# A wide opening over four k-tiles, earlier rotation tables, closer tap pacing, and a third fast pair at the end of a hybrid attention and convolution block

## The chip, the core and the metric

The kernel runs on one core of one Trainium2 chip. The metric is the device time of one launch in microseconds. TensorE (PE) multiplies, VectorE (DVE), ScalarE (ACT) and GpSimd (POOL) do the elementwise work, and SyncE (SP) issues most transfers. "The clock" below is the TensorE clock that the chip granted, as the profile shows it.

## What is computed

One layer on 256 rows of width 2048, all in float32. Only the shape of the work matters here:

```python
xn    = rms_norm(x, norm1_g)
proj  = xn @ w_in                          # 2048 x 5120: q, k, v, and two halves of a gated unit
q, k  = rope(rms_norm(q)), rope(rms_norm(k))
att   = rms_norm(diff_attention(q, k, v))  # 4 heads, each the difference of two softmaxes
u     = silu(layer_norm(causal_depthwise_conv(ga * sigmoid(gg), 31 taps)))
h     = x + concat(att, u) @ w_out         # 2048 x 2048
hn    = rms_norm(h, norm2_g)
y     = h + (silu(hn @ w_gate) * (hn @ w_up)) @ w_down   # hidden width 5632
```

## The kernel before

**Three products for one.** Every matrix operand is split into a rounded upper part (`hi`) and the remainder (`lo`). A k-tile (128 rows of a weight) times both row halves of the 256 rows (m = 0, 1) for one block of 512 columns takes six matmuls of 512 columns: `xhi*whi`, `xlo*whi` and `xhi*wlo`, each for both m (lines 364, 365 and 370). Per piece of weight, ACT casts `whi` (line 325) and DVE subtracts `wlo = raw - whi` (line 334). For some pieces ("by DMA") ACT writes `-whi` into `wlo` instead (line 328), and a transfer issued by POOL adds `raw` to it (line 329), so DVE has nothing to do.

**Chunks.** All weight work is a list of chunks in the order PE takes them. Before each chunk's matmuls, `run_chunks` emits the loads, casts and subtractions of the next ones: one chunk ahead in the opening (the first nine chunks), later two, or three casts and two subtractions ahead near a fast pair. There are five `raw` buffers, three of `whi` and three of `wlo`. SP takes its transfers in this order, one after the other, and a load waits there until its buffer is free. A chunk normally holds 512 KB: two k-tiles of 512 columns.

**The opening.** The first block of `w_in` (512 columns, 16 k-tiles) is cut into chunks of 1, 1, 2, 2, ... k-tiles. The transposed input `xt` is loaded between the weights as `XLOADS` says (before chunk 0 k-tile 0, before chunk 1 k-tiles 1 to 3, and so on), and `x_split` (lines 238 and 239) makes `xhi` on ACT and `xlo` on DVE. `x_norm` squares and adds the k-tiles in place, PE sums over partitions (line 495), and POOL makes the first norm's factor per row half.

**Side work in `w_in`.** `w_in` has ten blocks: four for the gated unit, four for k and q, two for v. What follows a block runs in generators that go one step on at each half chunk (`resume`). The convolution is 8 channel tiles of 30 taps on DVE (line 553). They sit in queues, and `run_side` emits them after each half chunk as long as a credit is positive: every half chunk adds `KTILE_US`, a tap takes away `TAP_US`, a `wlo` 0.568 per k-tile, and other DVE work what its author estimated. After the last tap, `conv_back` waits some half chunks, transposes `y` (line 574), normalizes, transposes again (line 611), and ACT and DVE make the operands `mchi` and `mclo` (lines 615 to 619) that `w_out` needs for its k-tiles 8 to 15. The tables that rotate q and k are made by POOL from `rt` and `gb` (lines 199 to 205), in `late_constants`.

**Gate, up and down.** The hidden width is taken in groups of 4, 4 and 3 blocks of 512. Each group is followed by its passes over `w_down`: for i = 0 and 1, one fast block gives 1024 of the 2048 output columns. A fast block has pairs (`s`), seven-product forms of 2 x 2 tiles with 21 matmuls, and plain chunks of two k-tiles for the left (`g`) or right (`u`) 512 columns, 12 matmuls each. One pair covers what one `g` and one `u` cover together. For a pair DVE makes four sums (lines 1019 to 1021) and the remainders `wlb` and `wlt` (1028 and 1029), ACT casts `wh` (1022 and 1025). The pairs' weights (`wb`, 1 MB) have two buffers; the sums have one. The order of the chunks is a string. In the last group, with 12 k-tiles, both blocks have two pairs: `gguusggsuu`, then `gggsgsuuuu`. The left-hand forms for the pairs are made by `make_down_forms` from copies of the activations (`raw_act`), 11 DVE operations per group.

**Results.** After a block's last chunk that is not `u`, `down_half` adds up the banks (lines 1156 to 1163) and POOL adds the left columns to `h` in DRAM by transfer (line 1210); `down_whole` does the rest (lines 1226 and 1238). Before the last block, the last 1024 columns of `h` are fetched (`hend`, line 1200), and the last block adds into them and writes the output.

Of the kernel before, what the change touches and what calls it, by code (L numbers as in the profile page):

```python
# [15 lines left out]
ALU = mybir.AluOpType  # L16
# [33 lines left out]

WARM = 17

XLOADS = {0: range(0, 1), 1: range(1, 4), 3: range(4, 8), 5: range(8, 12), 7: range(12, 16)}
XSQUARES = 4

XWHOLE = 40

FIRST_CUTS = (1, 1)
OPENING = KD // NK + 1

CONV_TILES = 2

# [5 lines left out]
COPY_LAG = 2  # L68
HL_BUFS = 3

KTILE_US = 1.30
TAP_US = 0.396
CHAIN_US = 0.127
LO_US = 0.568
# [12 lines left out]


HD = N // P
NDS = (4, 4, 2)  # L90
DORDERS = {4: (ORDER, ORDER), 3: ("gguusggsuu", "gggsgsuuuu")}
HD_LAG = 3
DOWN_BY_DMA = {4: (dict(g=(0, 1), u=(1,)),) * 2, 3: (dict(g=(), u=()),) * 2}

Q1, Q6, Q7, Q5, Q2, Q4, Q3, QX = range(8)

# [31 lines left out]
def tile_block(  # L128
# [52 lines left out]
    def late_loads():  # L181
        sp.dma_start(out=cw.rearrange("p c w -> p (c w)"), in_=conv_w)
        for t, v in ((gb, vecs[:2]), (lamv, vecs[2:])):
            sp.dma_start(out=t, in_=v.rearrange("(o v) d -> o v d", o=1).to_broadcast(list(t.shape)))
        sp.dma_start(out=rt, in_=rope.rearrange("(m p) c d -> p m c d", p=P))

    def late_constants():
        late_loads()
        while not normed:
            yield  # L190
        yield from lag(16)
        act.mul(cols[:, AT["sg"] : AT["sg"] + 2], cols[:, AT["sg"] : AT["sg"] + 2], 1.0 - LAMBDA_INIT)

        act.mul(gb[:, 0, :], gb[:, 0, :], 1.0 / math.sqrt(DH))
        hd = DH // 2
        for i, key in enumerate("qk"):
            for m in range(NM):
# [57 lines left out]
    def lag(n):  # L255
        for _ in range(n):
            yield
# [14 lines left out]
    def spend(us):  # L272
        credit[0] -= us
# [72 lines left out]
    def multiply(c):  # L346
# [42 lines left out]
        if c["done"]:  # L389
            start(c["done"](ps))  # L390

    def run_chunks():
        n = len(chunks)
        i = j = 0
        pairs = [k for k in range(n) if chunks[k].get("kind") == "s"]
        raws = [k for k in range(n) if chunks[k].get("kind") != "s" and not chunks[k].get("spare_raw")]
        loaded, split = set(), set()

        def load(k):
            if k not in loaded:  # L400
# [12 lines left out]
        def freed(side, t):  # L413

            which, bufs = ((raws, RAW_BUFS), (pairs, PAIR_BUFS))[side]
            if not ahead[side] or pairs[2] - 1 not in loaded:
                return None
            k = which[place[side][ahead[side][0]] - bufs]
            return k if k in split and (t >= k or not chunks[k]["by_dma"]) else None

        def load_freed(t):
            while True:
                ready = [(k, side) for side in range(2) if (k := freed(side, t)) is not None]
                if not ready:
                    return
                load(ahead[min(ready)[1]].pop(0))

        for t in range(n):
            hi_lead, lo_lead = lead(t)
            while j < min(i, t + 1 + lo_lead):  # L430
                split_next()
                j += 1
            load_freed(t)
            while i < min(n, t + 1 + hi_lead):
                load(i)
                for which in ahead:
# [19 lines left out]
    rstd1 = [const.tile([P, 1], F32, tag=f"rstd1_{m}", name=f"rstd1_{m}") for m in range(NM)]  # L456

    eps1 = [const.tile([P, 1], F32, tag=f"eps1_{m}", name=f"eps1_{m}") for m in range(NM)]

    def square_sum(src, accum, **kw):  # L460
        junk = pre.tile([P, N], F32, tag="junk", name="junk", bufs=1)
# [20 lines left out]
    def x_norm():  # L482
# [13 lines left out]
        yield  # L496
        ss = small.tile([P, NM], F32, tag="ss1", name="ss1")
        act.copy(ss, ps[:, :NM])
        for m in range(NM):
            rsqrt_mean(rstd1[m], ss[:, m : m + 1], -D / 2, EPS)  # L500
            pool.tensor_scalar(eps1[m], ss[:, m : m + 1], -2.0 * EPS / D, EPS * EPS, ALU.mult, ALU.add)
        yield
        normed.append(True)

# [14 lines left out]
    def glu_done(c0, nct, ps):  # L519
# [11 lines left out]
        for m in range(NM):  # L531
            u = pre.tile([P, HN], F32, tag="wt", name="u", bufs=4)
            dve.scalar_tensor_tensor(u[:, :w], ps[m][:, w:], rstd1[m], sig[m][:, :w], ALU.mult, ALU.mult)
            us.append(u)
        spend(0.25)
        yield from lag(3 if c0 else 1)
        yield from room(1)
# [29 lines left out]
    def conv_back(b):  # L567
# [32 lines left out]
        for b in range(2):  # L600
            for m in range(NM):
                act.activation(ytok[m, b], ytok[m, b], AF.Identity, bias=lnb[:, m : m + 1], scale=lnr[:, m : m + 1])
            yield
        for b in range(2):
            for t in range(NB // 2):
                yield from room(1)
# [254 lines left out]
    def transposed(j, aa):  # L861
        last = j + 1 in FIRSTS and NDS[group_of(j)[0]] < HD
        b = j - group_of(j)[1]
        for t in range(N // P // 2):
# [9 lines left out]
            if b < 2 and 2 * t < nd:  # L874
                if not b and not t:
                    raw_act[g] = ffn["pool"].tile([P, 2, nd, S], F32, tag="draw", name="raw_act")
                act.copy(raw_act[g][:, b, 2 * t : 2 * t + 2, :], pt)
                yield from lag(3 if last else 6)
                if b and 2 * t + 2 == nd:
                    start(make_down_forms(g))  # L880
                continue
            hi, lo = lhs_two("a", j * (N // P) + 2 * t)
            act.copy(hi, pt)
            yield from lag(1 if last else 2)
# [250 lines left out]

    def down_pass(g, j0, nb):
        k0 = j0 * HD
        nd = NDS[g]
        ks = [k for k in range(nb * HD) if k >= 2 * HD or k % HD >= nd]
        twos = [dict(ks=(k0 + a, k0 + b), rows=slice(k0 + a, k0 + b + 1, b - a), k=i)  # L1140
                for i, (a, b) in enumerate(zip(ks[::2], ks[1::2]))]
        for i, order in enumerate(DORDERS[nb]):
            n = 2 * i
            end = {}
            fast_block(order, [dict(p=p, rows=slice(k0 + p, k0 + p + HD + 1, HD)) for p in range(nd)], twos,
# [48 lines left out]
    def fetch_end():  # L1194

        t = ffn["pool"].tile([P, 7, NS, P], F32, tag="fhi", name="hend")
        t = t.rearrange("p a b c -> p (a b c)")
        for m in range(NM):
            hend.append(t[:, m * 2 * N : (m + 1) * 2 * N])
            sp.dma_start(out=hend[m], in_=hd[m][:, D - 2 * N :])  # L1200

    def down_half(g, n, q, end):
        gs, us = yield from bank_sums(q)
# [83 lines left out]
    def opening(i):  # L1287
        def begin():
            if i in XLOADS:
                x_load(XLOADS[i])  # L1290
            x_split(chunks[i]["ks"])
            if not i:
                start(x_norm())
        return begin

    def x_whole():
        for m in range(NM):
            sp.dma_start(out=h[m], in_=x[m * P : (m + 1) * P, :])

    for i in range(OPENING):  # L1300
        before[i] = opening(i)
    before[OPENING] = lambda: start(late_constants())
    before[XWHOLE] = x_whole
    run_chunks()

# [27 lines left out]
```

## Time and profile before

| | |
|---|---|
| median of 3 runs | 1036.13 us (1036.13 to 1036.54) |
| the profiled execution | 1035.99 us, its span 1034.2 us |
| PE busy | 1028.1 us, 4645 instructions |
| DVE busy | 927.3 us |
| ACT busy | 638.3 us |
| POOL busy | 108.7 us |
| bytes moved by DMA | 237.59 MB |

A line of the timeline has the start in us from the span's start, the duration, the engine, the line of the kernel, the operation, `output<-inputs` by tile name, the shape, how many instructions are merged, and in brackets the idle time before it and what ended it. Matmuls are pipelined, so their records overlap: one of 512 columns shows 0.39 us, but the next starts 0.227 us after it. PE's busy share therefore says little, and its stalls are read from the distance between starts. A line of stages has the stretch, and for each engine the busy time with the number of instructions, then the clock, the DMA share and GB/s.

### The profile page before, as it was taken

How to read it: one execution, taken by the hardware profiler on the slowest of the kernel's cores; microseconds unless marked ns; L12 is line 12 of the kernel's file. 1: busy time of each engine (PE TensorE's matmuls, PEld its weight loads, DVE VectorE, ACT ScalarE, POOL GpSimd, SP SyncE). 2: the span in 40 equal slices, each digit the busy share in tenths (PEclk: the TensorE clock that was granted, in tenths of full speed). 3: DMA queues.
4: the chain of work that ended last, by engine and by line, in shares of the span. 5: the costliest groups of instructions: out<-in, count | busy, mean ns of one | idle time of the engine just before them, and what ended most of it. 6: DMA issues, size and time to landing. Idle time of an engine off the chain costs nothing.

```text
span 1034.2 us, 13010 instructions
## 1 busy us (share of the span) xinstructions
PE 1028.1 (99%) x4645; PEld 848.9 (82%) x4645; DVE 927.3 (90%) x1126; ACT 638.3 (62%) x780; POOL 108.7 (11%) x147
## 2 busy tenths in 40 slices
PE   9999999999999999999999999999999999999998
PEld 7888888888888888888888888888888888888886
DVE  7899999989766699999999898989999989989887
ACT  7554656655666575677666556667657556667452
POOL 0130112111000100100102111001001111000010
PEclk9999999999999999999999999999999999999999
DMA  9657654553546677987989899879798979797773
GB/s 340 225 182 276 215 175 145 183 183 135 183 171 223 189 258 226 286 256 211 260 260 257 265 255 271 267 225 261 230 270 248 280 214 298 231 262 230 218 219 106
DMA packets 115664, 237.59 MB, mean 230 GB/s; under 512 B 7696, under 2 KB 8848, under 8 KB 115344
## 3 DMA queue, kind: packets, MB, share of 16 engines
q1 hardware_dynamic: 104720, 203.58, 59.0%
q0 software_dynamic: 10592, 33.04, 16.5%
q8 instruction: 36, 0.59, 0.2%
q14 instruction: 28, 0.23, 0.1%
q10 hardware_dynamic: 288, 0.16, 0.1%
HBM read 204.24 MB, written 9.44 MB: 207 GB/s over the span
## 4 chain that ended last, share of the span: by engine, by line
PE 96%; DVE 2%; DMA 1%; issue 1%; ACT 0%; SPq 0%; DVEq 0%
PE acc L364 11%; PE acc L365 11%; PE acc L370 11%; PE q L1067 11%; PE q L1068 11%; PE q L1073 11%; PE q L1048 9%; PE q L1046 9%; PE q L1047 9%; PE ps_a L871 1%; DVE wlo L334 1%; DMA raw<-in_w_in_dram 1%; PE ps_s L692 1%; PE ps_o L762 1%; DVE wlt L1029 0%
## 5 line engine op out<-in xcount | busy, mean ns | idle before, releaser
L325 ACT CAST whi<-raw 128x1024 fp32r<-128x1024 f32 (+1 forms) x257 | 266.4, 1047 | 149.7 <-PE acc L365 87.5
L334 DVE TENSOR_TENSOR wlo<-raw,whi 128x1024 fp32r<-128x1024 f32 (+1 forms) x211 | 254.6, 1217 | 37.9 <-ACT whi L325 37.8
L1025 ACT CAST wh<-wt 128x2048 fp32r<-128x2048 f32 x60 | 114.9, 1915 | 108.8 <-DVE wt L1021 108.7
L1029 DVE TENSOR_TENSOR wlt<-wt,wh 128x2048 fp32r<-128x2048 f32 x60 | 137.4, 2290 | 19.5 <-ACT wh L1025 19.4
L364 PE MATMUL acc<-whi,xhi 128*128 128x512 f32 x320 | 127.2, 398 | 0.7 <-ACT whi L325 0.6
L1067 PE MATMUL q<-whi,chi 128*128 128x512 f32 x320 | 125.2, 391 | 0.0
L365 PE MATMUL acc<-whi,xlo 128*128 128x512 f32 x320 | 125.1, 391 | 0.0
L1068 PE MATMUL q<-whi,clo 128*128 128x512 f32 x320 | 124.6, 389 | 0.0
L1046 PE MATMUL q<-wh,fhi 128*128 128x512 f32 x280 | 109.9, 392 | 0.0
L1047 PE MATMUL q<-wh,flo 128*128 128x512 f32 x280 | 108.9, 389 | 0.0
L1028 DVE TENSOR_TENSOR wlb<-wb,wh 128x1536 fp32r<-128x1536 f32 x60 | 105.1, 1751 | 1.1 <-ACT wh L1022 1.1
L553 DVE SCALAR_TENSOR_TENSOR y<-upad,cw,y 128x256 f32<-128x256 f32 x240 | 102.2, 485 | 2.2 <-ACT y L546 2.2
L329 POOL DMA_DIRECT2D wlo<-raw x46 | 39.8, 865 | 508.0 <-ACT wlo L328 283.4
L1022 ACT CAST wh<-wb 128x1536 fp32r<-128x1536 f32 x60 | 88.3, 1472 | 0.0
L370 PE MATMUL acc<-wlo,xhi 128*128 128x512 f32 x320 | 87.1, 393 | 0.0
L1073 PE MATMUL q<-wlo,chi 128*128 128x512 f32 x320 | 85.6, 389 | 0.0
L1067 PE MATMUL q<-whi,ahi 128*128 128x512 f32 x190 | 74.1, 390 | 0.0
L1068 PE MATMUL q<-whi,alo 128*128 128x512 f32 x190 | 74.0, 389 | 0.0
L1019 DVE TENSOR_TENSOR wt<-wb 128x1024 f32<-128x1024 f32 x60 | 73.1, 1218 | 0.0
L364 PEld LDWEIGHTS acc<-whi,xhi 128*128 128x128 f32 x320 | 60.3, 189 | 14.5 <-ACT whi L325 2.0
L365 PEld LDWEIGHTS acc<-whi,xlo 128*128 128x128 f32 x320 | 60.3, 188 | 12.3
L1073 PEld LDWEIGHTS q<-wlo,chi 128*128 128x128 f32 x320 | 60.1, 188 | 12.6
(253 smaller groups left out, 1836.3 us busy)
## 6 DMA issues: line engine op xcount, KB each, us to landing
raw<-in_w_in_dram SPq DMA_DIRECT2D x79, 512.0 KB, 4.7
raw<-in_w_gate_dram SPq DMA_DIRECT2D x48, 512.0 KB, 5.3
raw<-in_w_up_dram SPq DMA_DIRECT2D x48, 512.0 KB, 5.3
raw<-in_w_down_dram SPq DMA_DIRECT2D x48, 512.0 KB, 6.4
wlo<-raw POOLq DMA_DIRECT2D x46, 512.0 KB, 7.1
wb<-in_w_up_dram SPq DMA_DIRECT2D x40, 512.0 KB, 4.5
wb<-in_w_gate_dram SPq DMA_DIRECT2D x40, 512.0 KB, 5.8
wb<-in_w_down_dram SPq DMA_DIRECT2D x40, 512.0 KB, 6.0
```

The lines of the kernel that those rows point to most:

```text
L325: act.copy(c["hi"], c["raw"])
L334: dve.tensor_tensor(c["lo"], c["raw"], c["hi"].bitcast(F32), ALU.subtract)
L364: pe.matmul(ps[m], xhi[:, ms], hi[:, j, :], start=c["first"] and j == 0, stop=False)
L365: pe.matmul(ps[m], xlo[:, ms], hi[:, j, :], start=False, stop=False)
L370: pe.matmul(ps[m], xhi[:, ms], lo[:, j, :], start=False, stop=c["last"] and j == nk - 1)
L1025: act.copy(c["hi"][:, :SUMMED], c["t"])
L1029: dve.tensor_tensor(lot, c["t"], c["hi"][:, :SUMMED].bitcast(F32), ALU.subtract)
L1046: pe.matmul(ps, hi, c["hi"][:, w], start=bool(first), stop=False)
L1047: pe.matmul(ps, lo, c["hi"][:, w], start=False, stop=False)
L1067: pe.matmul(ps, xs[i][0][:, ms], hi[:, i, :], start=i == 0 and bool(c["first"].get(qs[m])), stop=False)
L1068: pe.matmul(ps, xs[i][1][:, ms], hi[:, i, :], start=False, stop=False)
L1073: pe.matmul(sum_bank(c, qs[m]), xs[i][0][:, ms], lo[:, i, :], start=False, stop=i == 1 and bool(c["last"].get(qs[m])))
```

## The change

There are six edits.

1. **Wide opening** (`WIDE = 4`). The first four k-tiles are multiplied for two blocks, 1024 columns. Chunks 0 and 1 are k-tile 0 for block 0 and for block 1; chunks 2 to 4 are k-tiles 1 to 3, each 1024 columns wide (`multiply_wide`, 12 matmuls); then come k-tiles 4 to 15 of block 0 and those of block 1. The sums of block 1 stay meanwhile in two of the four auxiliary banks. The opening has 11 chunks, and `XLOADS` brings `xt` as 1, 1, 2, 4, 4, 4 k-tiles.
2. **Rotation tables earlier.** `late_constants` starts with the opening's last chunk and goes on after 5 half chunks, without waiting for the first norm; `rt` is loaded in two parts.
3. **First norm.** `rstd1` and `eps1` are one tile of two columns each (3 POOL operations instead of 6), and ACT evaluates a sigmoid of a constant beforehand.
4. **Pacing.** `KTILE_US` goes from 1.30 to 1.335, and `conv_back` has one more `yield` ahead of the second transposes.
5. **Third pair.** The last block's order is `gsgsgsuuu`: three pairs, three `g`, three `u`. Its first two `g` chunks are by DMA. The forms of the last group are made for three pairs instead of two; the block before keeps two (`PASS_PAIRS`), and the third k-tile's plain operands are still made for it.
6. **Transfers cut.** `hend` comes in four transfers instead of two, `h` (chunk 40) in four instead of two.

```diff
-XLOADS = {0: range(0, 1), 1: range(1, 4), 3: range(4, 8), 5: range(8, 12), 7: range(12, 16)}
+WIDE = 4
+XLOADS = {0: range(0, 1), 2: range(1, 2), 3: range(2, 4), 5: range(4, 8), 7: range(8, 12), 9: range(12, 16)}
-FIRST_CUTS = (1, 1)
-OPENING = KD // NK + 1
+OPENING = 2 + WIDE - 1 + (KD - WIDE) // NK
-KTILE_US = 1.30
+KTILE_US = 1.335
-NDS = (4, 4, 2)
-DORDERS = {4: (ORDER, ORDER), 3: ("gguusggsuu", "gggsgsuuuu")}
+NDS = (4, 4, 3)
+PASS_PAIRS = ((4, 4), (4, 4), (2, 3))
+DORDERS = {4: (ORDER, ORDER), 3: ("gguusggsuu", "gsgsgsuuu")}
-DOWN_BY_DMA = {4: (dict(g=(0, 1), u=(1,)),) * 2, 3: (dict(g=(), u=()),) * 2}
+DOWN_BY_DMA = {4: (dict(g=(0, 1), u=(1,)),) * 2, 3: (dict(g=(), u=()), dict(g=(0, 1), u=()))}
...
     def late_constants():
         late_loads()
-        while not normed:
-            yield
-        yield from lag(16)
+        yield from lag(5)
...
+    def multiply_wide(c):
+        xhi, xlo = operand(c["xs"], c["k0"])
+        rows = [slice(m * P, (m + 1) * P) for m in range(NM)]
+        outs = [(accs["i", i][m], rows[m], slice(i * N, (i + 1) * N)) for i in range(2) for m in range(NM)]
+        for ps, ms, cs in outs:
+            pe.matmul(ps, xhi[:, ms], c["hi"][:, 0, cs], start=False, stop=False)
+            pe.matmul(ps, xlo[:, ms], c["hi"][:, 0, cs], start=False, stop=False)
+        resume()
+        run_side()
+        for ps, ms, cs in outs:
+            pe.matmul(ps, xhi[:, ms], c["lo"][:, 0, cs], start=False, stop=False)
+        resume()
+        run_side()
...
-        for m in range(NM):
-            rsqrt_mean(rstd1[m], ss[:, m : m + 1], -D / 2, EPS)
-            pool.tensor_scalar(eps1[m], ss[:, m : m + 1], -2.0 * EPS / D, EPS * EPS, ALU.mult, ALU.add)
+        act.activation(small.tile([P, 8], F32, tag="first", name="first"), neghalf, AF.Sigmoid)
+        rsqrt_mean(rstd1s, ss, -D / 2, EPS)
+        pool.tensor_scalar(eps1s, ss, -2.0 * EPS / D, EPS * EPS, ALU.mult, ALU.add)
...
                 act.activation(ytok[m, b], ytok[m, b], AF.Identity, bias=lnb[:, m : m + 1], scale=lnr[:, m : m + 1])
             yield
+        yield
...
-                act.copy(raw_act[g][:, b, 2 * t : 2 * t + 2, :], pt)
-                yield from lag(3 if last else 6)
-                if b and 2 * t + 2 == nd:
+                end = min(2 * t + 2, nd)
+                act.copy(raw_act[g][:, b, 2 * t : end, :], pt[:, : end - 2 * t])
+                if 2 * t + 2 <= PASS_PAIRS[g][0]:
+                    yield from lag(3 if last else 6)
+                if b and end == nd:
                     start(make_down_forms(g))
-                continue
+                if 2 * t + 2 <= PASS_PAIRS[g][0]:
+                    continue
...
+    for i in range(2):
+        block(w_in, i * N, range(1), fx, bkey=("i", i), last=False, spare=i == 1)
+    for k in range(1, WIDE):
+        block(w_in, [(0, 2 * N)], range(k, k + 1), fx, bkey=("i",), first=False, last=False)
+        chunks[-1]["multiply"] = multiply_wide
     for i, d in enumerate(done):
-        block(w_in, i * N, range(KD), fx, d, cuts=() if i else FIRST_CUTS)
+        if i < 2:
+            block(w_in, i * N, range(WIDE, KD), fx, d, bkey=("i", i), first=False)
+        else:
+            block(w_in, i * N, range(KD), fx, d)
```

More of the change, by code (lines that the diff above doesn't have):

```diff
@@ L184, in late_loads @@
             sp.dma_start(out=t, in_=v.rearrange("(o v) d -> o v d", o=1).to_broadcast(list(t.shape)))
-        sp.dma_start(out=rt, in_=rope.rearrange("(m p) c d -> p m c d", p=P))
+        for m in range(NM):
+            sp.dma_start(out=rt[:, m], in_=rope[m * P : (m + 1) * P])
     def late_constants():
         late_loads()
-        while not normed:
-            yield
-        yield from lag(16)
+        yield from lag(5)
         act.mul(cols[:, AT["sg"] : AT["sg"] + 2], cols[:, AT["sg"] : AT["sg"] + 2], 1.0 - LAMBDA_INIT)
@@ L455, in tile_block @@
     xT = {}
-    rstd1 = [const.tile([P, 1], F32, tag=f"rstd1_{m}", name=f"rstd1_{m}") for m in range(NM)]
-    eps1 = [const.tile([P, 1], F32, tag=f"eps1_{m}", name=f"eps1_{m}") for m in range(NM)]
+    rstd1s = const.tile([P, NM], F32, tag="rstd1", name="rstd1")
+    rstd1 = [rstd1s[:, m : m + 1] for m in range(NM)]
+    eps1s = const.tile([P, NM], F32, tag="eps1", name="eps1")
+    eps1 = [eps1s[:, m : m + 1] for m in range(NM)]
     def square_sum(src, accum, **kw):
@@ L534, in glu_done @@
             us.append(u)
+        if c0 == nct:
+            held[0] -= NM
         spend(0.25)
@@ L1137, in down_pass @@
         k0 = j0 * HD
[L1138 to L1141, printed above, removed]
         for i, order in enumerate(DORDERS[nb]):
+            nd = PASS_PAIRS[g][i]
+            ks = [k for k in range(nb * HD) if k >= 2 * HD or k % HD >= nd]
+            twos = [dict(ks=(k0 + a, k0 + b), rows=slice(k0 + a, k0 + b + 1, b - a), k=i)
+                    for i, (a, b) in enumerate(zip(ks[::2], ks[1::2]))]
             n = 2 * i
@@ L1199, in fetch_end @@
             hend.append(t[:, m * 2 * N : (m + 1) * 2 * N])
-            sp.dma_start(out=hend[m], in_=hd[m][:, D - 2 * N :])
+        for a in range(0, 2 * N, N):
+            for m in range(NM):
+                sp.dma_start(out=hend[m][:, a : a + N], in_=hd[m][:, D - 2 * N + a : D - N + a])
     def down_half(g, n, q, end):
@@ L1290, in begin @@
                 x_load(XLOADS[i])
-            x_split(chunks[i]["ks"])
+            x_split([k for k in chunks[i]["ks"] if k not in xT])
             if not i:
                 start(x_norm())
+            if i == OPENING - 1:
+                start(late_constants())
         return begin
@@ L1297, in x_whole @@
         for m in range(NM):
-            sp.dma_start(out=h[m], in_=x[m * P : (m + 1) * P, :])
+            for a in range(0, D, D // 2):
+                sp.dma_start(out=h[m][:, a : a + D // 2], in_=x[m * P : (m + 1) * P, a : a + D // 2])
     for i in range(OPENING):
         before[i] = opening(i)
-    before[OPENING] = lambda: start(late_constants())
     before[XWHOLE] = x_whole
```

## The prediction

> **What bounds the kernel now.** I read the page's first part, then the chain of waits by engine, then stages.
>
> ```profile
> PE 1028.1 (99%) x4645; PEld 848.9 (82%) x4645; DVE 927.3 (90%) x1126; ACT 638.3 (62%) x780; POOL 108.7 (11%) x147
> ...
> PE 96%; DVE 2%; DMA 1%; issue 1%; ACT 0%; SPq 0%; DVEq 0%
> ```
>
> PE sets the time from the first weights to the last, so a change pays only where it removes matmuls or closes a hole between them. Everything on DVE, ACT and POOL counts only where PE comes to wait for it. There are two places with holes: the opening and the last pass. 0.2% of this kernel, about what a measurement can tell from no change, is 2.07 us.
>
> The opening, in the timeline:
>
> ```profile
> 4.64 0.62 ACT L325 CAST whi<-raw 128x512 fp32r<-128x512 f32 x1 [0.90 <-DMA raw<-in_w_in_dram]
> 5.31 0.80 PE L364 MATMUL acc<-whi,xhi 128*128 128x512 f32 x1
> ...
> 6.86 0.63 PE L370 MATMUL acc<-wlo,xhi 128*128 128x512 f32 x2
> 7.39 0.62 ACT L325 CAST whi<-raw 128x512 fp32r<-128x512 f32 x1 [1.13 <-DMA raw<-in_w_in_dram]
> 8.06 0.49 PE L364 MATMUL acc<-whi,xhi 128*128 128x512 f32 x1 [0.57 <-ACT whi L325]
> ...
> 8.72 1.05 ACT L325 CAST whi<-raw 128x1024 fp32r<-128x1024 f32 x1
> 9.83 0.50 PE L364 MATMUL acc<-whi,xhi 128*128 128x512 f32 x1
> 12.68 0.39 PE L364 MATMUL acc<-whi,xhi 128*128 128x512 f32 x1
> ...
> 17.21 1.07 PE L370 MATMUL acc<-wlo,xhi 128*128 128x512 f32 x4
> 18.12 0.39 PE L364 MATMUL acc<-whi,xhi 128*128 128x512 f32 x1
> ```
>
> Four matmuls take 18.12 - 17.21 = 0.91 us, 0.227 each; a k-tile (6) is 1.36 us, a chunk of 12 is 2.72. Chunk 0 begins at 5.31. Its last two matmuls begin at 6.86, so it is over at 6.86 + 0.45 = 7.31, but chunk 1 starts at 8.06: a hole of 0.75. Chunk 1 would end at 9.42, chunk 2 starts at 9.83 (0.41); it would end at 12.55, chunk 3 starts at 12.68 (0.13). Together 1.28 us, and the casts begin as their weights land. From 12.68 on starts follow each other without a hole.
>
> **Edit 1, wide opening.** Matmuls neither come nor go. What changes is how many bytes lie ahead of each. A k-tile of `xt` is 128 KB, one of weights for a block 256 KB. Before, SP had asked for 384 KB when chunk 0's weights were in (cast at 4.64), for 1024 KB with chunk 1's (7.39) and 1536 KB with chunk 2's (8.72), so 512 KB take 1.33 us. Now it is 640 KB with chunk 1's: between 384 KB at 4.64 and 1024 KB at 7.39 that is 5.74, cast by 6.4, ahead of 7.31, no hole. With chunk 2's (k-tile 1, both blocks) it is 1280 KB: 8.72 - 256 x 1.33 / 512 = 8.06, cast over at 9.11, matmul at 9.15. Chunk 1 ends at 7.31 + 1.36 = 8.67, so a hole of 0.48 is left. Chunk 2 then runs to 11.87. Chunk 3's come after another 768 KB, 2.0 us later, so cast by 11.1: no hole, and each following chunk gains on PE, since 512 KB of weights and 128 of `xt` take 1.66 us and feed 2.72. Gain 1.28 - 0.48 = 0.80 us. Bounds: if chunk 2's weights come no earlier than before (8.72), it starts at 9.83 with as many matmuls behind it as before, and only the 0.13 ahead of chunk 3 is gained; if they come by 7.6 all of 1.28. I take 0.80. DVE, with two `xlo` and a `wlo` per chunk, does the same in the six chunks after as before, and less in the wide ones.
>
> **Edits 2 and 3.** The tables' POOL operations and the factor stand ahead of nothing on PE; the first is needed by the first k block. Block 0 ends two chunks later than before, so its gated unit and the first taps come 4 half chunks later. The new transfers of `rt` and, in edit 6, of `h` and `hend` add issue time on SP, where loads run several chunks ahead. Taken as 0, covered by PE's matmuls; without that cover the taps would end late, which is the last rival.
>
> **Edit 4, pacing.** Between first and last tap the credit must pay 240 x 0.396 = 95.0 for taps and 13.9 for other work (8 x 1.65 for q and k, 3 x 0.25, 0.3, 4 x 0.8, less 4 x 0.9). A half chunk brings 1.30 less 0.568 for its share of `wlo`: 108.9 / 0.732 = 149 half chunks, from the 24th to the 172nd. Now it is 0.767: 142 half chunks from the 28th, to the 169th; but the last two refunds of 0.9 come only at the 170th and 171st, so carried through it ends at the 171st. One half chunk is won, the added `yield` spends it, and the second transposes come where they came. What stands behind them:
>
> ```profile
> 280.43 0.43 DVE L619 TENSOR_TENSOR mclo<-z,mchi 128x256 fp32r<-128x256 f32 x1
> ...
> 281.51 0.48 PE L364 MATMUL acc<-whi,mchi 128*128 128x512 f32 x1
> ```
>
> The first two operands are ready at 280.86, 0.65 us ahead of PE. Cost 0; a half chunk later would cost 1.36 - 0.65 = 0.7, one earlier gains nothing.
>
> **Edit 5, third pair.** The last block has 3 x 21 + 6 x 12 = 135 matmuls instead of 2 x 21 + 8 x 12 = 138: 0.68 us. It also moves the pairs, and DVE is what they wait for:
>
> ```profile
> 987.32 3.49 DVE L334 TENSOR_TENSOR wlo<-raw,whi 128x1024 fp32r<-128x1024 f32 x3
> 992.38 0.69 DVE L1158 TENSOR_TENSOR sum<-q,sum 128x512 f32<-128x512 f32 x1 [1.57 <-ACT sum L1156]
> ...
> 996.37 1.22 DVE L334 TENSOR_TENSOR wlo<-raw,whi 128x1024 fp32r<-128x1024 f32 x1
> 998.11 1.29 DVE L1226 TENSOR_TENSOR sum<-q,sum 128x512 f32<-128x512 f32 x2 [0.52 <-PE q L1073]
> ...
> 1006.52 0.39 PE L1046 MATMUL q<-wh,dhs 128*128 128x512 f32 x1
> ...
> 1007.03 0.50 PE L1048 MATMUL q<-wlt,dhs 128*128 128x512 f32 x1
> 1007.37 0.40 PE L1046 MATMUL q<-wh,dls 128*128 128x512 f32 x1
> ...
> 1008.03 1.22 DVE L1019 TENSOR_TENSOR wt<-wb 128x1024 f32<-128x1024 f32 x1
> 1010.62 1.75 DVE L1028 TENSOR_TENSOR wlb<-wb,wh 128x1536 fp32r<-128x1536 f32 x1
> 1012.69 2.29 DVE L1029 TENSOR_TENSOR wlt<-wt,wh 128x2048 fp32r<-128x2048 f32 x1 [0.31 <-ACT wh L1025]
> ...
> 1014.42 0.39 PE L1047 MATMUL q<-wh,dls 128*128 128x512 f32 x1
> 1014.90 1.22 DVE L334 TENSOR_TENSOR wlo<-raw,whi 128x1024 fp32r<-128x1024 f32 x1
> 1015.03 0.50 PE L1048 MATMUL q<-wlt,dhs 128*128 128x512 f32 x1 [0.23 <-DVE wlt L1029]
> 1015.37 0.40 PE L1046 MATMUL q<-wh,dls 128*128 128x512 f32 x1
> ```
>
> The second pair's third product starts 0.61 us after its neighbour instead of 0.23, the next after 0.34 instead of 0.23, and at 1007.03 another 0.16 is lost: 0.65 us of holes for late `wlt`. A pair takes DVE from 1008.03 to 1014.90, 6.87 us: 2.59 for the sums, 1.67, 0.4 of waiting for ACT, 2.21. PE takes 4.76 for it.
>
> In the new order (in the clock of the old trace; the first pair stood three chunks into the block, which therefore starts at 1006.52 - 8.16 = 998.36): the third `wlo` of 987.32 falls away (by DMA), so DVE is free at 989.6 and makes the first pair's sums by 992.2, ahead of the bank sums at 992.38. At 996.37 follow its remainders, 3.87 us, to 1000.24. PE needs them for the third product, at 998.36 + 2.72 + 0.46 = 1001.54. The adds of line 1226 run to 1001.44, the second pair 6.87 to 1008.31; needed at 1001.08 + 4.76 + 2.72 + 0.46 = 1009.02. The third `g`'s `wlo` 1.14, the third pair to 1016.32; needed at 1008.56 + 4.76 + 2.72 + 0.46 = 1016.50. All three are met, the last by 0.2. The `u` remainders and the final sums then have 8 us of PE. So the 0.65 goes too, less 0.2 that I leave for the thin last margin: gain 0.68 + 0.65 - 0.2 = 1.13. The best end is 1.33.
>
> Two transfers could spoil it:
>
> ```profile
> wlo<-raw POOLq DMA_DIRECT2D x46, 512.0 KB, 7.1
> ```
> ```profile
> q1 hardware_dynamic: 3, 0.01, 2.3%
> ...
> hend<-hd SPq DMA_DIRECT2D x2, 512.0 KB, 10.8
> raw<-in_w_down_dram SPq DMA_DIRECT2D x1, 512.0 KB, 7.8
> ```
> ```profile
> q0 software_dynamic: 459, 1.11, 107.7%
> ...
> wb<-in_w_down_dram SPq DMA_DIRECT2D x2, 512.0 KB, 10.7
> ```
> ```profile
> q0 software_dynamic: 397, 0.74, 57.3%
> q1 hardware_dynamic: 426, 1.30, 50.4%
> ```
>
> The first fence is the page's list of transfers (count, KB each, us to landing), the others the DMA view of 997:1000, of 802:808 (SP's queue q1 has no line there) and of 1002:1009 (packets, MB). The second `g` by DMA has its `wlo` buffer at 995.64, when PE has done the last chunk but one of the block before; with ACT's negation (about one cast, 1.05) the transfer starts at 997 and lands 7.1 later, 1004.1. It is needed at 1005.84 + 1.81 = 1007.65: covered. On POOL's queue the adds of line 1210 wait behind it, and nobody on PE waits for those. The third pair's `wb` is the other. Its buffer comes free with the first pair's `wlb`, at 998.04, and its sums begin at 1009.45: 11.4 us for 1 MB. The transfers issued around 998 took 7.8 and 10.8, those of 806 10.7: just enough, cost 0. With 11.8 it would cost 0.4.
>
> Trainium skill, "DMA: Bandwidth & Descriptors", section "Queues, rings and completion order": each engine takes its queues in turn, packet by packet. The two windows do not look like that: with POOL's queue full, SP's moved 3 packets in 3 us and none in 6. By the rule, 1 MB at half the opening's pace of 1.33 us per 512 KB takes 5.3 us and lands at about 1005 (an estimate by that page); the sum would be the same with 4 us to spare, and by the windows it has nearly nothing to spare.
>
> The forms for three pairs cost 11 DVE operations of 384 columns instead of 256, in a block where DVE has idle time, and ACT two small copies: 0.
>
> **Sum.** 0.80 + 1.13 = 1.93 us off the profiled execution's 1035.99 (span 1034.2 and 1.8 around it): 1034.06. The median of the runs lies 0.14 above that execution, so 1034.2 us, 0.19% less, just inside what counts as no change.
>
> **Rivals.**
> *Both holes close entirely.* Chunk 2's weights land by 7.6 and no pair is late: 1.28 + 1.33 = 2.61, 1033.5 us. For it: from 384 KB at 4.64 on at 1.33 us per 512 KB, 1280 KB would be there at 6.97. Against it: the 640 KB up to 7.39, which were slower.
> *The wide opening does not pay.* The first megabyte is slow whatever its order, chunk 2 still starts at 9.83: 0.13 + 1.13, 1034.9 us. For it: 4.64 to 7.39 brought only 640 KB.
> *The third pair starves (the other side).* SP's queue gets nothing until POOL's is empty. Behind 997 there stand a `wlo` of 512 KB and four adds of 256 KB on POOL's. From 999 on, at the second window's 1.11 MB in 6 us, the 1.5 MB last 8.3 us, and 1 MB at 1.33 us per 512 KB follows: 999 + 8.3 + 2.7 = 1010, a stall of 0.4 after the margin. With the adds at the third window's 0.74 MB in 7 us it is 999 + 2.8 + 9.5 + 2.7 = 1014, a stall of 4.4, and the kernel takes 1036.13 - 0.80 - 1.13 + 4.4 = 1038.6. It ends slower than before once the load lands after 1011.5. For it: the first two windows, where SP's queue stood still. Against it: the third, where both moved, and the adds of line 1238, which now come 3 us later.
> *The taps do not come closer.*
>
> ```profile
> 50.00:75.00 25.00, 25.00 (x114) 20.69 (x113) 25.00 (x45) 12.77 (x18) 8.66 (x14) 1.00 0.57 189
> ...
> 150.00:175.00 25.00, 25.00 (x120) 20.84 (x119) 23.68 (x44) 14.93 (x36) 5.17 (x6) 1.00 0.58 186
> ...
> 225.00:250.00 25.00, 24.96 (x118) 20.34 (x117) 22.46 (x51) 16.05 (x33) 2.94 (x7) 1.00 0.38 128
> ```
>
> DVE (third busy time) is full from 50 to 75. If it can take no more taps, they end 4 half chunks late, the `yield` adds one: 5 x 1.36 - 0.65 = 6.2 us at the first `mchi`, 1040.4 us. Against it: 4 half chunks' worth, 4 x 0.732 = 2.9 us, has to be caught up, and the later two stages alone leave DVE idle for 3.9 us.
>
> **How the numbers follow.** Forecast 0.48 (own range 1033.7 to 1034.8), holes closed 0.16, wide opening for nothing 0.13, starved pair 0.15 (spread from 1034.5 to 1038.6), taps 0.08. Faster by over 0.2% (under 1034.06): 0.16 and nearly half of the forecast, 0.38. Slower (over 1038.2): the taps and a fifth of the starved pair, 0.11. Same: 0.51. Range 1033.3 to 1036.7: it leaves out the taps, the worse half of the starved pair, and a little below.
>
> **What would show it.** Chunk 1 following chunk 0 at 7.3, chunk 2 between 8.7 and 9.8; three pairs in the last 31 us whose `wlt` products show no gap over 0.1; `wb` of the third pair landing before its first sum; the first `mchi` product at the same distance behind its `mclo`. A wait of PE for `wlt` or of DVE for `wb` after 1005, or for `mclo` near 280, would prove me wrong.

## The result, and the profile after

The changed kernel takes 1034.06 us (median of 11 runs, 1033.32 to 1034.45); the kernel before took 1036.67 on the same chip (11 runs). The ratio is 0.9975, with an interval of 0.9968 to 0.9983: 2.6 us less, a little beyond the 0.2% that the prediction takes as the least that can be told; the near end of the interval, 0.17%, lies inside it. Timed again later, beside each other, the two gave 1034.02 and 1036.36, ratio 0.9972 (0.9960 to 0.9983). The forecast was 1034.2, with 1.93 us off, 0.19%: just inside "no change", which had half of the chance, where the median shows just outside, on the faster side. Two executions below, one of e6 (1139.80 us) and one of e11 (2109.99 us), fell into a slow state and are left out of the medians.

The profiled execution of the changed kernel took 1033.71 us. First part of its page, and the shares of its chain of waits by engine:

```profile
PE 1026.1 (99%) x4642; PEld 849.3 (82%) x4642; DVE 928.7 (90%) x1127; ACT 643.2 (62%) x785; POOL 103.0 (10%) x146
...
PE 99%; DMA 1%; SPq 0%; ACT 0%; issue 0%; DVE 0%
```

Three matmuls fewer (4642 for 4645), and DVE, which held 2% of the chain, is down to 0%. What is left is PE and the first transfers. The only wait of PE after the warm-up (engine, line, what it waited for: total us, times, longest):

```profile
PE acc L397 <- ACT whi L325: 0.6, 1, 0.6
```

The opening, in the timeline (start, us, engine, line, what; in brackets the idle time before it and its cause):

```profile
4.11 0.62 ACT L325 CAST whi<-raw 128x512 fp32r<-128x512 f32 x1 [0.43 <-DMA raw<-in_w_in_dram]
4.89 0.78 PE L364 MATMUL acc<-whi,xhi 128*128 128x512 f32 x1
...
7.08 0.40 PE L364 MATMUL acc<-whi,xhi 128*128 128x512 f32 x1
...
8.13 1.05 ACT L325 CAST whi<-raw 128x1024 fp32r<-128x1024 f32 x1 [0.75 <-DMA raw<-in_w_in_dram]
...
9.23 0.50 PE L397 MATMUL acc<-whi,xhi 128*128 128x512 f32 x1 [0.60 <-ACT whi L325]
...
14.82 0.39 PE L397 MATMUL acc<-whi,xhi 128*128 128x512 f32 x1
```

Chunk 1 follows chunk 0 without a hole (7.08); one hole is left, ahead of the first wide chunk, and none after it. A product after a wait shows 0.34 us to the next start instead of 0.23; it isn't counted as a hole. The pairs of the last block, from the same timeline:

```profile
988.51 1.22 DVE L1041 TENSOR_TENSOR wt<-wb 128x1024 f32<-128x1024 f32 x1
...
991.28 0.69 DVE L1180 TENSOR_TENSOR sum<-q,sum 128x512 f32<-128x512 f32 x1
...
996.94 2.28 DVE L1051 TENSOR_TENSOR wlt<-wt,wh 128x2048 fp32r<-128x2048 f32 x1
...
1000.43 0.39 PE L1070 MATMUL q<-wlt,dhs 128*128 128x512 f32 x1
...
1004.99 2.29 DVE L1051 TENSOR_TENSOR wlt<-wt,wh 128x2048 fp32r<-128x2048 f32 x1 [0.31 <-ACT wh L1047]
...
1006.64 1.49 ACT L1044 CAST wh<-wb 128x1536 fp32r<-128x1536 f32 x1 [0.74 <-DMA wb<-in_w_down_dram]
...
1007.91 0.39 PE L1070 MATMUL q<-wlt,dhs 128*128 128x512 f32 x1
1008.33 1.22 DVE L1041 TENSOR_TENSOR wt<-wb 128x1024 f32<-128x1024 f32 x1
...
1012.98 2.29 DVE L1051 TENSOR_TENSOR wlt<-wt,wh 128x2048 fp32r<-128x2048 f32 x1 [0.31 <-ACT wh L1047]
...
1015.39 0.43 PE L1070 MATMUL q<-wlt,dhs 128*128 128x512 f32 x1
```

Each `wlt` ends ahead of the product that uses it: 999.22 for 1000.43, 1007.28 for 1007.91, 1015.27 for 1015.39. No PE row there has a bracket. The third pair's weights come just in time: ACT's cast waits 0.74 us for them until 1006.64, and DVE's sums, at 1008.33, don't wait.

**Where the time went.** All openings have the same 36 matmuls in their first chunks, so the start of the 37th can be compared (15.40 before, 14.82 after), and so can that of the last matmul of the kernel (1030.30 and 1027.87). Up to the 37th, 0.58 us were won; between the two points 1.85, of which 1.33 is the third pair (0.68 for three matmuls and 0.65 of holes) and 0.5 lies thinly spread over 970 us; the end, where only results leave, gave 0.15 back.

### The profile page after: what moved, and what is told of

It reads as the page before. It is cut to its first block, busy times and chain, and to the rows that moved or that the text cites. A ratio compares the mean times of both kernels' runs of the same rounds, so it can differ in the third digit from the quotient of the medians.

```text
span 1031.9 us, 13028 instructions
## 1 busy us (share of the span) xinstructions
PE 1026.1 (99%) x4642; PEld 849.3 (82%) x4642; DVE 928.7 (90%) x1127; ACT 643.2 (62%) x785; POOL 103.0 (10%) x146
## 4 chain that ended last, share of the span: by engine, by line
PE 99%; DMA 1%; SPq 0%; ACT 0%; issue 0%; DVE 0%
PE q L1089 11%; PE q L1090 11%; PE q L1095 11%; PE acc L370 11%; PE acc L365 11%; PE acc L364 11%; PE q L1070 9%; PE q L1069 9%; PE q L1068 9%; PE ps_a L890 1%; DMA raw<-in_w_in_dram 1%; PE ps_s L711 1%; PE ps_o L781 1%; PE ps_h L832 0%; PE ps_qk L692 0%; PE acc L397 0%
## 5 line engine op out<-in xcount | busy, mean ns | idle before, releaser
L334 DVE TENSOR_TENSOR wlo<-raw,whi 128x1024 fp32r<-128x1024 f32 (+1 forms) x207 | 249.6, 1216 | 39.9 <-ACT whi L325 39.9
L1051 DVE TENSOR_TENSOR wlt<-wt,wh 128x2048 fp32r<-128x2048 f32 x61 | 139.7, 2290 | 19.8 <-ACT wh L1047 19.7
L364 PE MATMUL acc<-whi,xhi 128*128 128x512 f32 x308 | 122.7, 398 | 0.0
L365 PE MATMUL acc<-whi,xlo 128*128 128x512 f32 x308 | 120.5, 391 | 0.0
L370 PE MATMUL acc<-wlo,xhi 128*128 128x512 f32 x308 | 83.8, 393 | 0.0
L1089 PE MATMUL q<-whi,ahi 128*128 128x512 f32 x182 | 71.1, 391 | 0.0
L1090 PE MATMUL q<-whi,alo 128*128 128x512 f32 x182 | 70.9, 390 | 0.0
L1089 PEld LDWEIGHTS q<-whi,chi 128*128 128x128 f32 x320 | 60.1, 188 | 12.3
L1090 PEld LDWEIGHTS q<-whi,clo 128*128 128x128 f32 x320 | 60.1, 188 | 12.2
```

Source lines behind the costliest of these rows:

```text
L334: dve.tensor_tensor(c["lo"], c["raw"], c["hi"].bitcast(F32), ALU.subtract)
L364: pe.matmul(ps[m], xhi[:, ms], hi[:, j, :], start=c["first"] and j == 0, stop=False)
L365: pe.matmul(ps[m], xlo[:, ms], hi[:, j, :], start=False, stop=False)
L370: pe.matmul(ps[m], xhi[:, ms], lo[:, j, :], start=False, stop=c["last"] and j == nk - 1)
L1051: dve.tensor_tensor(lot, c["t"], c["hi"][:, :SUMMED].bitcast(F32), ALU.subtract)
L1089: pe.matmul(ps, xs[i][0][:, ms], hi[:, i, :], start=i == 0 and bool(c["first"].get(qs[m])), stop=False)
```

## Experiments

Each ratio is to the kernel before, on the same chip; its medians were 1036.40 (e1 to e4), 1036.24 (e5 to e8) and 1036.36 (e9 to e12).

**e1: edit 5 alone, in the kernel before; e2: the changed kernel without it.** (The new lines of `glu_rest` and `down_pass` go with the table below.)

```diff
-NDS = (4, 4, 2)
-DORDERS = {4: (ORDER, ORDER), 3: ("gguusggsuu", "gggsgsuuuu")}
+NDS = (4, 4, 3)
+PASS_PAIRS = ((4, 4), (4, 4), (2, 3))
+DORDERS = {4: (ORDER, ORDER), 3: ("gguusggsuu", "gsgsgsuuu")}
-... 3: (dict(g=(), u=()),) * 2}
+... 3: (dict(g=(), u=()), dict(g=(0, 1), u=()))}
```

> The kernel before with edit 5 alone (third pair). Theory A, the parts add up and each closes its own hole: 1.1 to 1.3 us less than before (0.68 for three matmuls, 0.45 to 0.65 for the late remainders), ratio about 0.9988. Rival B, the gain comes from the earlier tables and the pacing: within 0.3 us of before. Rival C, starved pair: slower than before, with a wait of DVE for wb after 1005.

> The changed kernel without edit 5. Theory A: 0.6 to 1.3 us less than before (the opening and what little drifts with it), ratio about 0.999, and the hole of 0.39 at the last pair's third product is back. Rival B: nearly all of the gain stays, 2 us or more less than before.

e1: 1034.92 us, 0.9987 (0.9978 to 0.9996), 1.5 less. e2: 1035.31, 0.9989 (0.9980 to 0.9998), 1.1 less. Together that is 2.6, the whole gain; so far as intervals of 0.9 us to either side can tell, the two parts don't touch each other. In e2 the hole for a late `wlt` is back; PE's waits of e2, and the timeline at the place:

```profile
PE acc L396 <- ACT whi L324: 1.4, 1, 1.4
...
PE q L1066 <- DVE wlt L1047: 0.2, 1, 0.2
```
```profile
1013.70 0.39 PE L1065 MATMUL q<-wh,dls 128*128 128x512 f32 x1
1014.32 0.50 PE L1066 MATMUL q<-wlt,dhs 128*128 128x512 f32 x1 [0.23 <-DVE wlt L1047]
```

The third product starts 0.62 us after its neighbour instead of 0.23, as before the change.

**e3: the old pacing in the changed kernel; e4: without the added `yield`.**

```diff
-KTILE_US = 1.335
+KTILE_US = 1.30
```

> The changed kernel with KTILE_US back at 1.30. Theory A, the pacing only keeps the normalization in time: by the credit's account the last tap comes at half chunk 177 instead of 171, the first mchi product waits, and the kernel is 2 to 7.5 us slower than the changed one, 0 to 5 us slower than before. Rival, DVE was full anyway and the pacing moves no tap: the same as the changed kernel within 0.3 us.

> The changed kernel without the added yield. Theory A: second transposes half a chunk (1.36 us) earlier, PE is not waiting for them, so the same as the changed kernel within 0.3 us. Rival: the yield keeps PE from waiting for ACT's normalized rows, without it 0.4 us or more slower with a wait of PE at the second transposes.

e3: 1040.70 us, 1.0044 (1.0030 to 1.0058), 6.7 more than the changed kernel. PE's waits of e3, and its timeline where they end:

```profile
PE ps_ln L630 <- ACT upad L620: 2.8, 2, 2.4
PE acc L364 <- DVE mchi L637: 1.6, 1, 1.6
```
```profile
285.21 0.79 PE L364 MATMUL acc<-whi,mchi 128*128 128x512 f32 x1 [1.64 <-DVE mchi L637]
```

The wide opening lets the taps begin four half chunks later (the first starts at 44.4 us, where it was 39.1). With the old pace they end later too: the last starts at 270.5, at 262.0 in the changed kernel and at 264.3 in the kernel before. PE waits first for the transposes' input and then for `mchi`. It isn't a full DVE that holds the taps back: over 75 to 100 us the changed kernel keeps it busy all the time, and e3 leaves it idle for 0.81 us. The rows of e3 and of the changed kernel (DVE's busy time is the one of x45 and x48):

```profile
75.00:100.00 25.00, 25.00 (x114) 20.72 (x113) 24.19 (x45) 11.80 (x14) 0.00 (x0) 1.00 0.67 232
```
```profile
75.00:100.00 25.00, 25.00 (x114) 20.72 (x113) 25.00 (x48) 11.81 (x14) 0.00 (x0) 1.00 0.72 242
```

So the credit is short, and the new pace gives the time back. The changed kernel where the operands are used:

```profile
278.95 0.42 DVE L638 TENSOR_TENSOR mclo<-z,mchi 128x256 fp32r<-128x256 f32 x1
...
280.68 0.48 PE L364 MATMUL acc<-whi,mchi 128*128 128x512 f32 x1
```

The first two operands are ready at 279.37, 1.31 us ahead of PE, where it was 0.65. e4: 1033.97 us, 0.9978 (0.9969 to 0.9988): the `yield` costs nothing that can be measured.

**e5: the last block's two `g` remainders by DVE again instead of by DMA.**

```diff
-DOWN_BY_DMA = {4: ..., 3: (dict(g=(), u=()), dict(g=(0, 1), u=()))}
+DOWN_BY_DMA = {4: ..., 3: (dict(g=(), u=()),) * 2}
```

> The changed kernel with the last block's first two g remainders on DVE again (no transfer for them). Theory A, DVE's margin at the last pairs is 0.2 to 0.7 us: the second of them, 1.14 us, comes between the first and the second pair, so the second pair's third product waits about 0.5 us and the third pair's another 0.5; 0.5 to 1.1 us slower than the changed kernel. Rival, DVE has room: the same within 0.2 us. Rival, the transfers cost more than they save: faster.

1035.88 us, 0.9997 (0.9988 to 1.0006): about 2 us of the changed kernel's 2.6 are lost again, where 0.5 to 1.1 were expected. PE's waits of e5, and DVE's rows:

```profile
PE q L1070 <- DVE wlt L1051: 1.5, 2, 1.3
```
```profile
986.81 3.49 DVE L334 TENSOR_TENSOR wlo<-raw,whi 128x1024 fp32r<-128x1024 f32 x3
990.22 1.22 DVE L1041 TENSOR_TENSOR wt<-wb 128x1024 f32<-128x1024 f32 x1
...
992.81 0.68 DVE L1180 TENSOR_TENSOR sum<-q,sum 128x512 f32<-128x512 f32 x1
...
1001.86 1.21 DVE L334 TENSOR_TENSOR wlo<-raw,whi 128x1024 fp32r<-128x1024 f32 x1
...
1007.64 2.29 DVE L1051 TENSOR_TENSOR wlt<-wt,wh 128x2048 fp32r<-128x2048 f32 x1 [0.31 <-ACT wh L1047]
```

I had taken the first remainder as harmless and counted the second alone. But between the three `wlo` of 986.81 and the second pair no bracket stands in DVE's list: the bank sums follow directly on the pair's sums (at 992.81 here, 991.28 in the changed kernel), so 1.14 us more in front moves everything behind. Both count, 2.28 us, against a margin of 0.63 at the second pair: 1.65 by this sum, 1.48 in the trace, and 0.38 more at the third pair.

**e6: the rotation tables and the first norm's factor as before (edits 2 and 3 undone).**

```diff
-        yield from lag(5)
+        while not normed:
+            yield
+        yield from lag(16)
...
-        rsqrt_mean(rstd1s, ss, -D / 2, EPS)
+        for m in range(NM):
+            rsqrt_mean(rstd1[m], ss[:, m : m + 1], -D / 2, EPS)
```

> The changed kernel with edits 2 and 3 undone: tables after the first norm and 16 half chunks, one chunk later start, factor by six POOL operations, no sigmoid beforehand. Theory A: PE waits for none of it, the same as the changed kernel within 0.3 us. Rival B: 0.5 us or more slower.

1033.9 us, 0.9979 (0.9970 to 0.9988): the same as with them.

**e7 and e10: k-tile 1 in two chunks of 256 KB as well, wide chunks from k-tile 2 on; e11: k-tile 2 too.** `XLOADS` moves along.

```diff
+CUT = 2          # e11: 3
-    for i in range(2):
-        block(w_in, i * N, range(1), fx, bkey=("i", i), last=False, spare=i == 1)
-    for k in range(1, WIDE):
+    for k in range(CUT):
+        for i in range(2):
+            block(w_in, i * N, range(k, k + 1), fx, bkey=("i", i), first=not k, last=False, spare=i == 1)
+    for k in range(CUT, WIDE):
```

> The changed kernel with the second k-tile too cut into two chunks, one for each block (256 KB each) instead of one of 512 KB. Theory A, the hole that is left (0.77 us ahead of the first wide chunk) is the wait for 512 KB: the first half comes 0.6 us earlier and is cast in 0.62 instead of 1.05, the hole closes, 0.5 to 0.8 us less than the changed kernel. Rival, the early transfers are slow whatever their order: under 0.2 us.

> The opening with k-tile 1 in two chunks of 256 KB too, once more, now on the same chip as the changed kernel. If the wide chunk is too large for the second place, it is 0.6 to 1.0 us faster than the changed kernel and its runs lie closer together, as they did. If the 0.8 us that stood between them was the chip of that day, they are equal within 0.2 us.

> k-tile 2 in two chunks of 256 KB as well. With k-tile 1 cut, one hole of 0.30 us was left, ahead of the first wide chunk at 11.37 us, whose 512 KB landed at 10.17. The first half would land near 9.5 and be cast by 10.2, ahead of 11.07, and the other half is needed only at 12.4. So the hole closes: up to 0.3 us less than with two, no more. Rival: each transfer more takes about 0.47 us of SP's issuing, and the x columns and weights that follow come later; then a hole of 0.2 us or more opens ahead of a wide chunk between 13 and 20 us, and the time is the same or longer.

e7: 1033.23 us, 0.9970 (0.9959 to 0.9982). e10, the same kernel, beside the changed kernel's 1034.02 on one chip: 1033.41 (1033.18 to 1033.56), 0.6 less. e11: 1033.17, 0.9966 (0.9954 to 0.9979), 0.2 less than e10, which the runs don't separate. These are the fastest versions; each beats both kernels. In e11 the hole has moved one k-tile on, to the first chunk of 512 KB; that row of e11, and the one of e10:

```profile
13.88 0.50 PE L398 MATMUL acc<-whi,xhi 128*128 128x512 f32 x1 [0.32 <-ACT whi L326]
```
```profile
11.72 0.50 PE L398 MATMUL acc<-whi,xhi 128*128 128x512 f32 x1 [0.70 <-ACT whi L326]
```

So I was half right on e11: the hole at k-tile 2 closed, and the rival's hole ahead of the next chunk opened (0.48 us later than an even pace). Whether it comes from the extra transfers wasn't separated.

**e8: three pairs in the block before the last, too.**

```diff
-PASS_PAIRS = ((4, 4), (4, 4), (2, 3))
-DORDERS = {4: (ORDER, ORDER), 3: ("gguusggsuu", "gsgsgsuuu")}
+PASS_PAIRS = ((4, 4), (4, 4), (3, 3))
+DORDERS = {4: (ORDER, ORDER), 3: ("gusgsgsuu", "gsgsgsuuu")}
-... 3: (dict(g=(), u=()), dict(g=(0, 1), u=()))}
+... 3: (dict(g=(0, 1), u=()),) * 2}
```

> The changed kernel with three pairs in the last group's first block too (gusgsgsuu, its first two g by transfer). Theory A: three matmuls less, 0.68 us, if DVE keeps up; its first pair stands two chunks into the block, beside the sums of the block before, so up to 1 us of that may come back as late remainders: between 0.68 less and 0.4 more than the changed kernel. Rival: DVE is the bound of the whole last pass, slower by more than 1 us.

1047.87 us, 1.0111 (1.0097 to 1.0124), 14 more than the changed kernel: a clear miss on the rival's side, far beyond the size that I gave it. PE's waits of e8, and one of DVE's in 1012:1030:

```profile
PE ps_a L890 <- DVE alo L907: 5.0, 1, 5.0
PE q L1070 <- DVE wlt L1051: 3.2, 2, 1.6
PE q L1068 <- DVE alo L907: 1.4, 1, 1.4
```
```profile
DVE wt L1041 <- DMA wb<-in_w_down_dram: 2.2, 1, 2.2
```

PE's three waits add up to 9.6 us. An earlier start of the pairs puts their sums and remainders in front of `alo`, on which PE's next operands depend (two pairs' work on DVE, then `alo` at 979.73, then PE at 980.47). That is DVE's order in the first of the two blocks; in the last one DVE itself waits. The last line is the starved third pair of the prediction: here DVE did wait 2.2 us for `wb`, and PE 1.6 us for the `wlt` made from it.

**e9: the changed kernel again; e12: the loads of `hend` six half chunks later.**

```diff
-            fetch_end()
             yield from lag(6)
+            fetch_end()
```

> The changed kernel once more, beside the kernel before on the same chip, to price the three runs that follow. My theory: 2.2 to 2.7 us less than before, a ratio of 0.9974 to 0.9979, as when it was first timed. If its hole ahead of the first wide chunk is a matter of chance in each execution, as six traces of the same opening suggest (from under 0.25 to 1.57 us), it is again another than 0.77 us. If it belongs to the kernel, it is 0.77 within 0.1.

> The changed kernel with the four loads of h's last columns (1 MB on SP's queue, issued at 998.1 to 1000.8) six half chunks later. They stand behind the third pair's 1 MB of weights on the same queue. If a queue moves its transfers one after the other, the two halves of that load still land 7.0 and 9.0 us after issue (within 0.7). If transfers of one queue share the engines, they land 2 us or more sooner, and the next load (14.6 us in the changed kernel) too. The time is the same within 0.3 us in either case: the loads are first used at 1023.2 by DVE and land 10 to 14 us after issue, by about 1020, and the third pair's sums did not wait for its weights.

e9: 1034.02 us (7 runs). Its opening:

```profile
4.83 0.50 PE L364 MATMUL acc<-whi,xhi 128*128 128x512 f32 x1
...
7.23 0.61 PE L370 MATMUL acc<-wlo,xhi 128*128 128x512 f32 x2
...
8.31 1.04 ACT L325 CAST whi<-raw 128x1024 fp32r<-128x1024 f32 x1 [0.76 <-DMA raw<-in_w_in_dram]
...
9.41 0.50 PE L397 MATMUL acc<-whi,xhi 128*128 128x512 f32 x1 [1.57 <-ACT whi L325]
```

The hole is 1.73 us, where the first trace of this kernel had 0.77; yet both executions took about the same time (1034.06 and 1033.71), for the wide chunk starts at 9.41 and 9.23. The two first chunks ran at full pace at once here (0.23 us from start to start) and at half pace there. What ran sooner only waited longer: the landing of the wide chunk's 512 KB sets the start, and the size of the hole says little.

e12: 1033.99 us, 0.9974 (0.9963 to 0.9984), the same time. The transfers of e9 and of e12 in 996:1002 (count, KB each, median us to landing):

```profile
wb<-in_w_down_dram SPq DMA_DIRECT2D x2, 512.0 KB, 8.2
...
raw<-in_w_down_dram SPq DMA_DIRECT2D x1, 512.0 KB, 14.5
```
```profile
wb<-in_w_down_dram SPq DMA_DIRECT2D x2, 512.0 KB, 8.2
...
raw<-in_w_down_dram SPq DMA_DIRECT2D x1, 512.0 KB, 12.9
```

The edit moved less than I had meant. By the timeline `hend` is issued from 999.91 on instead of 998.42, and all that changes is its order with `raw`, issued at 998.60 instead of 1001.76. So 1.5 MB stand behind `wb` in both, and that it lands as late doesn't tell whether transfers of one queue share the engines: the question of e12 stays open. What the run does show is that the place counts: `raw`, 3.2 us sooner in the queue, lands at about 1011.5 instead of 1016.3.

## Why the prediction was right, and where by luck

**Bound, and the third pair (forecast 1.13, found 1.33 in the trace, 1.5 in e1).** The mechanism held row by row. The changed trace runs 1.1 us ahead of the old one at that point, and with this shift the first pair's sums, forecast from 989.6, begin at 988.51. The margins were put at 1.3, 0.7 and 0.2 us and are 1.21, 0.63 and 0.12. The last was thin but held, so the 0.2 that I kept back for it was not needed: the best end, 1.33. The remainders by DMA carry more of this than the prediction says: without them 2 us go (e5).

**Wide opening (forecast 0.80).** Chunk 1 came as forecast, and the wide chunk, forecast at 9.15, started at 9.23. But nine traces with this opening have it between 8.91 and 9.68, with a median of 9.50, and the 37th matmul at 14.48 to 15.27, median 15.08. The old opening has it at 15.40 and, in e1, at 15.81. That is 0.3 to 0.7 us instead of 0.80, inside the bounds of 0.13 and 1.28. The mis-sized step is "512 KB take 1.33 us, ... 8.06": one trace's landings stood for all, and in other executions the same bytes came up to 0.5 later. Chunk 3's weights came later than forecast as well: 2.63 us behind chunk 2's (casts at 8.13 and 10.76, both waiting for their transfer) instead of 2.0, so they were cast by 11.81, 0.28 ahead of their first product at 12.09. Of the two rivals on the opening, "both holes close" is out. "Nothing gained" is out by the median, but the slowest of the nine (e12, 9.68 and 15.27) gains just its 0.13 against the first trace of the old opening. No run moves the `xt` loads back without the wide blocks, so the two weren't separated. e7 shows that what was left could be had: with only 256 KB asked for in the third place, too, 0.6 to 0.8 us more go.

**Edits 2, 3 and 6, and the pacing (forecast 0).** e6 shows it for 2 and 3 (`rt` stayed in two parts), e4 for the `yield`; edit 6 was not undone by itself. The second transposes did come where they came (276.68 for 277.49, with PE 0.8 us ahead by then). The first `mchi` product wasn't at the same distance behind its `mclo`, though: 1.31 us instead of 0.65, since ACT had now normalized all rows before those transposes (by 275.86; before, the last two operations began at 277.44); it changes nothing. The rival of the late taps came near the right price for the wrong reason, and by luck: 6.2 us in the prediction, 6.7 in e3, of which the two waits shown are 4.4. DVE, full from 50 to 75 us after the change too, takes 36 taps there instead of 33 and does catch up; what is short in e3 is credit, not DVE.

**The missing 0.4.** The forecast has no term for 0.2 to 0.55 us that the changed kernels save between the 37th matmul and the last pair of the block before the last (988.16 before, 987.06 after), a little at many places. e2 has it (0.43), e1 hasn't (0.06), e6 (0.55) and e4 (0.30) keep it. So it isn't edit 5, the tables, the factor or the `yield`. Nor does it grow only where the other edits act: a product of the first gate block that starts at 365.40 us before starts at 364.62 after, one of the second group's passes over `w_down` at 840.17 starts at 839.15, so 0.24 of it arises between the two, where no edit acts. Its cause stays open. By luck it stands against what the opening gave less, so the total came out nearer than its parts: forecast 0.80 + 1.13, found, between the two profiled executions, 0.58 + 1.33 + 0.5 less the 0.15 of the end, 2.3 us. The medians stand 2.3 to 2.6 apart.

**The starved pair and the queues.** The transfer view of the changed kernel, in 997:999, 999:1001, 1001:1004 and 1004:1007 (packets, MB, share of 16 engines; q0 is POOL's queue, q1 SP's):

```profile
q0 software_dynamic: 64, 0.26, 71.3%
...
q0 software_dynamic: 60, 0.25, 101.6%
q1 hardware_dynamic: 17, 0.03, 5.2%
...
q1 hardware_dynamic: 381, 0.75, 90.7%
q0 software_dynamic: 20, 0.02, 5.5%
...
q0 software_dynamic: 158, 0.30, 55.9%
q1 hardware_dynamic: 244, 0.46, 50.9%
```

SP's queue gets next to nothing until about 1001, while POOL's moves its 512 KB for `wlo`; then SP's has the engines to itself for 3 us, although POOL's adds have been issued since 997; then both move. So the rival ("nothing until POOL's is empty", landing at 1010 to 1014 in the old trace's clock, 1.1 us less in this one) was wrong after its first 4 us. The two halves of `wb` were issued at 997.1 and 997.5 with a median of 8.0 us to landing, and the cast that waited for the second began at 1006.64: they landed at about 1004.0 and 1006.6. The taking of turns in the Trainium skill ("DMA: Bandwidth & Descriptors", section "Queues, rings and completion order") fits the last window and not the two before it. The prediction's estimate by that rule was 1005 for both, which is 1003.9 in this trace's clock; its 5.3 us, counted from the issue at 997.1, would end at 1002.4 already. Neither the rival nor that rule says why the adds, issued first, stand aside from 1001 to 1004; that stays open. The margin at DVE was 1.7 us (1006.6 for 1008.33): wider than the "nearly nothing" by the old windows. In e8 it is gone with the same transfers around `wb`: in 1011:1014, as long after its `wlo` transfer as 1001:1004 here, POOL's queue moves 94 packets beside SP's 271, and the second half lands 13.0 us after its issue instead of about 9. Why the queues share differently there stays open.

## What to carry to other kernels

Where PE is full, the last block's price is found by writing out the other engine's list in order and comparing each end with the product that uses it; here that came out within 0.1 us at three places. An instruction is harmless on such an engine only if a bracket (idle time) stands between it and the point in question, however far ahead it is (e5, e8). At the start of a kernel price the landing of each piece from several executions, not from one, compare the starts behind a hole and not the hole, and keep the pieces small until PE has work in hand.

## What the runs showed that I had not expected

The first matmuls run at half pace in some executions (0.4 to 0.6 us from start to start until 6.4 us) and at full pace in others (0.23 from 5.2 on in e9), and the total doesn't care, since the next landing decides. The granted clock reads 1.00 over 4 to 8 us in both, so these traces don't tell why.

A hole costs more than its length when PE has waited long. In e3, where PE was busy for 0.87 of the 5 us up to 285, the first product after the wait took 0.79 us against 0.48 in the changed kernel, and the granted clock over the next 5 us was 0.50. In e8 it was 0.91 over 960:1000, which holds the wait of 5.0 us. It is 1.00 in the changed kernel at both places; PEclk is the figure after the five engines, in e3's row and in e8's. After the single waits of 1.48 us in e5 and of 1.59 in e8's last block, products started 0.23 us apart again from the second on.

```profile
285.00:290.00 5.00, 4.79 (x13) 3.84 (x14) 1.20 (x4) 0.32 (x2) 0.00 (x0) 0.50 0.00 0
```
```profile
960.00:1000.00 40.00, 32.01 (x134) 25.50 (x133) 33.03 (x33) 21.26 (x19) 1.75 (x2) 0.91 0.68 202
```
